# Moving 212 Strassen weight sums from GpSimd to VectorE, with a reordered opening and three re-placed pieces of vector work

## The chip, the cores and the metric

The program runs on one core of a Trainium2 chip. The metric is the device time of one execution in microseconds, the median of several runs. The engines are TensorE (PE, with its weight loads as PEld), VectorE (DVE), ScalarE (ACT) and GpSimd (POOL); SyncE (SP) only issues DMA. Each engine runs its own instructions in order and waits on semaphores of the others.

## The reference

One inference step of a one-layer encoder, float32, on 1,024 prompt tokens and 32 sample tokens (1,056 together, each 1,024 wide), and 256 memory tokens. Cut to its stages:

```python
def encoder_layer(h, ...):
    u = rms_norm(h, norm1)
    z = u @ w_in + b_in                       # q, k, v, gates of three branches
    o_h = hgrn2_recurrence(...)               # 4 heads, normed, gated
    h_m = mlstm_recurrence(q, k, v, i_pre, log_sigmoid(f), ...)   # 4 heads
    p = softmax(einsum(q_x, mem_k) * XA_DH ** -0.5)   # 4 heads, 256 memory tokens
    merged = sum of sigmoid(gate_b) * (branch_b @ w_branch[b])
    h = h + merged @ w_out
    up_g, up_v = split(rms_norm(h, norm2) @ w_up)     # 2 x 2,816
    conv = causal depthwise conv of width 3 over up_g
    h = h + (gelu(conv) * up_v) @ w_down
y = rms_norm(h, final_norm)
mem_k, mem_v = split(rms_norm(mem, mem_norm) @ w_mem_kv)
m_t = max over time of the mLSTM's running exponents  # the "rows" below
```

## The kernel before, in words

Activations lie transposed: channels on the 128 partitions, the 1,056 tokens as four column quarters of 264. Every product is three matmuls (`mm3`, L221 to L223): hi by hi, lo by hi and hi by lo, where `split` (L225) makes the hi part of an operand by an ACT cast (L226) and the lo part by a DVE subtraction (L227).

The large projections (`w_in` as `z_m1_m2`, `w_up` as `u0` to `u21`) use Strassen's scheme: seven products of 2x2 blocks in place of eight. For one pair of weight column blocks `operands` (L250) loads four weight quarters (L214, issued by SP into a ring of four buffers), forms four sums of them (`add`, L258) and splits the seven operands. 53 such sets give 212 sums. `seven` (L289) runs the products in the order 1, 2, 6, 5, 7, 3, 4 and adds them up from PSUM on ACT (L307, L309) and DVE (L311). The token side has the same seven operands (`put`, `put_sums`, L344 to L368), made once for `u1` (the normed input) and once for `n2` (the normed residual).

The stages in order of time: memory keys and values (`pm`, L527, eight weight blocks `wm0` to `wm7`) and, among them, the token norm with its transposes (`xp`, L469); the first z pairs (`z_35`, `z_33`) with cross-attention; HGRN2; the mLSTM's rows (`mlstm_rows`, L1043: 4x1056 scans over time on DVE) while gate projections run; the mLSTM heads; branch projections and gates; `wout_job` (L1294), which adds each block to the residual `acc` (L1317), squares it (L1322) and sums the squares (`sq`, L1323); `rstd_cols` (L317), whose matmuls `n21b` (L329) read `sq`; the up stage with a depthwise conv (L1371, L1374) and a gate product on POOL (`vt`, L1377, L1378), stored to DRAM as `h_d`; `down` (L1469), which loads `h_d` back (`hr`, L1462), splits it into `h` and multiplies by `w_down` (`pd`); the final norm.

The order of the work comes from `Flow` (L62): a clock kept by hand in which `fl.unit` adds the planned TensorE time of a piece, and generators (`x_norm`, `mlstm_rows`, the norms) are resumed when the clock has passed the wait that their `yield` names. `prep` and `ahead` (L195, L199) set how many weight operands are made ahead. The text is written in that order, and from it the instructions of each engine get a fixed order.

## Time and profile before

| what | value |
|---|---|
| median of 3 runs | 1861.42 us (1857.13 to 1862.22) |
| the profiled execution | 1859.81 us |
| its span | 1857.9 us |
| PE busy in the span | 1803.6 us (97%) |
| DVE, ACT, POOL busy | 1177.4, 842.6, 490.6 us |
| mean granted clock | 0.989 |

The span runs from the first to the last instruction of the profiled execution; 1.9 us of that execution's time lie around it. Busy time counts an engine's instructions; idle time of PE is put down to the instruction on another engine that released it last. The granted clock is a share of the full 2.4 GHz: 1.00 is that, 0.50 is 1.2 GHz, and a window between has some of both.

### The profile page before, as it was taken

Reading aid. Unit: us, or ns where it says so; the run is one execution under the profiler, and the core shown is the slowest. Engines: PE = TensorE matmul, PEld = TensorE weight load, DVE = VectorE, ACT = ScalarE, POOL = GpSimd, SP = SyncE. Lnnn points to the kernel's source line nnn. Section 1 sums busy time; section 2 is a strip of 40 time slices with the busy share of each in tenths; the row PEclk is TensorE's granted clock in tenths of the full one; section 3 lists DMA queues with packets and bytes.
Section 4 is the critical chain, followed back from the end, with each engine's and each line's share of the span. In section 5 each row is a group of like instructions: output and inputs, shape, how many; then the busy total and the mean of one; then the engine's idle time right before and its main releaser. Section 6 shows DMA issues by size and latency. Waiting matters only on the chain.

```text
span 1857.9 us, 35747 instructions
## 1 busy us (share of the span) xinstructions
PE 1803.6 (97%) x14249; PEld 1770.5 (95%) x14249; DVE 1177.4 (63%) x2265; ACT 842.6 (45%) x1779; POOL 490.6 (26%) x535
## 2 busy tenths in 40 slices
...
GB/s 299 43 53 64 87 57 64 62 55 55 81 86 111 57 67 66 62 79 206 320 384 248 119 106 67 98 70 87 72 84 70 87 78 127 287 146 144 133 97 127
DMA packets 99687, 213.95 MB, mean 115 GB/s; under 512 B 10788, under 2 KB 34724, under 8 KB 99520
## 3 DMA queue, kind: packets, MB, share of 16 engines
...
## 4 chain that ended last, share of the span: by engine, by line
PE 86%; DVE 7%; DMA 2%; ACT 2%; issue 1%; POOL 1%; SPq 0%; DVEq 0%; ACTq 0%; POOLq 0%
PE pd L221 4%; PE pd L222 4%; PE pd L223 4%; PE pb L222 2%; PE pb L223 2%; PE pb L221 2%; PE po L221 1%; PE po L222 1%; PE po L223 1%; DMA hr<-h_d 1%; DMA mems<-in_mem 1%; DMA wm<-in_w_mem 0%; PE fin L806 0%; PE z_55c0q L221 0%; PE z_2c0q L221 0%
## 5 line engine op out<-in xcount | busy, mean ns | idle before, releaser
L1377 POOL TENSOR_TENSOR vt<-cv,vt 128x1024 f32<-128x1024 f32 x22 | 53.4, 2425 | 107.3 <-ACT cv L1376 107.3
L1374 DVE SCALAR_TENSOR_TENSOR cv<-cb,par,cv 128x1058 f32<-128x1058 f32 x44 | 61.3, 1392 | 1.4
L1273 DVE TENSOR_TENSOR g<-pb,g 128x352 f32<-128x352 f32 x72 | 37.0, 521 | 23.8 <-PE pb L223 18.2
L527 PE MATMUL pm<-memg,wm 128*128 128x256 f32 x128 | 31.7, 398 | 9.4 <-DVE memg L427 7.9
L227 DVE TENSOR_TENSOR h<-hr,h 128x528 fp32r<-128x528 f32 x44 | 31.7, 746 | 13.0 <-ACT h L226 12.6
L527 PEld LDWEIGHTS pm<-memg,wm 128*128 128x128 f32 x128 | 24.5, 199 | 12.9 <-DVE memg L427 7.9
L325 POOL MEMSET fn11rs<- 128x3 f32 x1 | 0.1, 100 | 131.7 <-DVE fn00a L175 131.7
L226 ACT CAST h<-hr 128x528 fp32r<-128x528 f32 x44 | 26.5, 631 | 17.5 <-DMA hr<-h_d 15.2
L1448 POOL TENSOR_TENSOR y<-y,fn10b 128x264 f32<-128x264 f32 x4 | 3.8, 980 | 110.5 <-ACT fn10b L1442 110.5
L611 ACT ACTIVATE gt<-gt 128x1056 f32<-128x1056 f32 x24 | 26.0, 1088 | 10.8 <-DVE gt L311 10.8
L1275 DVE TENSOR_TENSOR old<-old,g 128x352 f32<-128x352 f32 x48 | 25.1, 523 | 6.0 <-DMA old<-part 5.1
L612 POOL DMA_DIRECT2D g_d<-gt x24 | 13.4, 557 | 50.3 <-ACT gt L611 47.7
L1322 ACT ACTIVATE sqt<-acc 128x264 f32<-128x264 f32 x28 | 11.8, 423 | 32.0 <-DVE acc L1317 29.5
L1376 ACT ACTIVATE cv<-cv 128x1058 f32<-128x1058 f32 x22 | 24.0, 1090 | 4.0 <-DVE cv L1374 2.0
L226 ACT CAST mgh<-old 128x264 fp32r<-128x264 f32 x32 | 12.4, 412 | 27.9 <-DVE old L1275 27.9
L1325 POOL DMA_DIRECT2D h_d<-acc x8 | 6.1, 759 | 71.9 <-DVE acc L1317 71.9
L1317 DVE TENSOR_TENSOR acc<-acc,po 128x264 f32<-128x264 f32 x32 | 13.6, 424 | 16.9 <-PE po L223 16.9
L1517 DVE TENSOR_TENSOR y<-y,pd 128x264 f32<-128x264 f32 x32 | 12.7, 426 | 10.1 <-PE pd L223 10.1
L1371 DVE TENSOR_SCALAR cv<-cb,par 128x1058 f32<-128x1058 f32 x22 | 18.5, 841 | 0.1
L1367 POOL COPY ffo<-cb 128x2 f32<-128x2 f32 x22 | 5.5, 252 | 45.7 <-DVE cb L311 45.7
L1323 DVE TENSOR_TENSOR sq<-sq,sqt 128x264 f32<-128x264 f32 x28 | 13.2, 473 | 6.3 <-ACT sqt L1322 6.3
L1531 ACT ACTIVATE fqt<-y 128x264 f32<-128x264 f32 x28 | 11.3, 419 | 12.9 <-DVE y L1517 12.9
...
## 6 DMA issues: line engine op xcount, KB each, us to landing
...
```

The lines of the kernel that those rows point to most:

```text
L221: PE.matmul(out, lh, rh, start=first and i == 0, stop=False, skip_group_check=part)
L222: PE.matmul(out, lh, rl, start=False, stop=False, skip_group_check=part)
L223: PE.matmul(out, ll, rh, start=False, stop=last and i == n - 1, skip_group_check=part)
L226: S.copy(hi, src)
L227: V.tensor_tensor(out=lo, in0=src, in1=hi.bitcast(F32), op=ALU.subtract)
L527: PE.matmul(ps[:, 0:NM], w[:, 4 * a + k], mg[a][:, k], start=a + k == 0, stop=a + k == 4)
L611: S.activation(t, t, AF.Sigmoid)
L1273: V.tensor_tensor(out=gt[:, c], in0=ps[:, 0:GW], in1=gt[:, c], op=ALU.mult)
L1275: V.tensor_tensor(out=old[:, c], in0=old[:, c], in1=gt[:, c], op=ALU.add)
L1374: V.scalar_tensor_tensor(out=cv, in0=cb[:, tap:tap + n], scalar=col(C_CW + tap * NF + i), in1=cv, op0=ALU.mult, op1=ALU.add)
L1376: S.activation(cv, cv, AF.Gelu_apprx_tanh)
L1377: G.tensor_tensor(out=vt[:, 0:TP], in0=cv[:, 0:TP], in1=vt[:, 0:TP], op=ALU.mult)
```

## The change

Five edits.

1. `add` issues its 212 additions on VectorE (`V`) where it used GpSimd (`G`).
2. The opening's loads on SP go in another order: first x0, the gain row and x1, then the halves of memT and wm0, then x2 to x4, wm1, x5 to x8, wm2, the two blocks of memory rows, wm3 and on. Squares, reciprocal roots and scaling of the token rows (`x_scale`) are written where the rows are loaded, not one chunk after another in `x_norm`.
3. `mlstm_rows` is cut by seven `yield`s, so that other work may stand between its steps, and begins later in the planned clock (9.0 in place of 3.0).
4. The operands of the first up block (`u0`, first half) are registered inside the loop over `wout_job`, at its sixth block of the second half, with homes of their own for both raw weights; its last two operands are registered behind the loop.
5. In `down` the `hr` loads of the next three steps are issued ahead of the weight loads, and the residual loads (`y`) come at step 4 and not at step 0.

The core of the diff:

```diff
         def add(n, a, b, out=None):
...
-            G.tensor_tensor(out=out, in0=a, in1=b, op=ALU.add)
+            V.tensor_tensor(out=out, in0=a, in1=b, op=ALU.add)
             return out
...
+                            if i in homes:
                                 if not kh:
-                                    t = other[0](f"{nm}r1").bitcast(F32)
+                                    t = homes[i](f"{nm}r{i}").bitcast(F32)
                                 raws[i, kh] = t[:, kh * HK:(kh + 1) * HK]
                                 nc.sync.dma_start(raws[i, kh], src)
...
             return go
-        first = [prep(1 if n >= len(other) else 0.25, make(p)) for n, p in enumerate(ORD)][0]
-        return first, ops
...
+        entries = []
+        def register(part):
+            entries.extend(prep(1 if n >= len(other) else 0.25, make(ORD[n])) for n in part)
+        register(range(7 if later is None else len(other)))
+        if later is not None:
+            later.append(lambda: register(range(len(other), 7)))
+        return entries, ops
...
+    LOADS = ((2, 3, 4), (5, 6, 7, 8), (9, 10)) + ((),) * 5
...
                 nc.sync.dma_start(t, I["w_mem"][i])
-                for j in ((), (2, 3, 4), (5, 6), (7, 8))[i] if i < 4 else ():
-                    x_load(j)
-                if i == 2:
-                    for j in range(2):
-                        nc.sync.dma_start(mem_s[j], I["mem"][j * P:(j + 1) * P])
+                for j in LOADS[i]:
+                    load_rows(j)
+                for j in LOADS[i]:
+                    if j < NC:
+                        x_scale(j)
...
             nc.scalar.dma_start(par, I["par"])
             x_load(0)
+            grow.append(slot("grow", F32)[:, 0:D])
+            nc.sync.dma_start(grow[0], I["g1"].broadcast_to([P, D]))
+            x_load(1)
             for a in range(2):
                 c = slice(a * HK, (a + 1) * HK)
                 nc.sync.dma_start(mem_f[a], I["memT"][a])
                 nc.sync.dma_start(t[:, c], I["w_mem"][0][:, c])
-            grow.append(slot("grow", F32)[:, 0:D])
-            nc.sync.dma_start(grow[0], I["g1"].broadcast_to([P, D]))
-            x_load(1)
+            for j in LOADS[0]:
+                load_rows(j)
+            for j in (0, 1, *LOADS[0]):
+                x_scale(j)
             fl.start(x_norm(), 0.0, key="u")
...
+    def x_scale(i):
+        n = CHUNKS[i][1]
+        if not xss:
+            xss.append(mp.tile([P, 16], F32, tag="ssn", name="xss", bufs=3))
+            G.memset(xss[0], 1.0)
+        ss, x = xss[0], x_t[i]
+        junk = mp.tile([P, D], mybir.dt.bfloat16, tag="pe", name=f"junk{i}", bufs=4)
+        S.activation(junk[:n], x[:n], AF.Square, accum_out=ss[:n, i:i + 1])
+        y = rsqrt(ss[:, i:i + 1], 1, f"x{i}", 1.0 / D)
+        V.scalar_tensor_tensor(out=x[:n], in0=x[:n], scalar=y[:n, 0:1], in1=grow[0][:n], op0=ALU.mult, op1=ALU.mult)
...
         for i, (t0, n) in enumerate(CHUNKS):
             x = x_t[i]
-            junk = mp.tile([P, D], mybir.dt.bfloat16, tag="pe", name=f"junk{i}", bufs=4)
-            S.activation(junk[:n], x[:n], AF.Square, accum_out=ss[:n, i:i + 1])
-            y = rsqrt(ss[:, i:i + 1], 1, f"x{i}", 1.0 / D)
-            V.scalar_tensor_tensor(out=x[:n], in0=x[:n], scalar=y[:n, 0:1], in1=grow[0][:n], op0=ALU.mult, op1=ALU.mult)
-            yield 0.0, 1.6, None
             for kh in range(2):
...
         S.activation(e, e, AF.Ln, bias=1.0)
+        yield 0.0, 6.5, None
         V.scalar_tensor_tensor(out=x, in0=x, scalar=0.0, in1=e, op0=ALU.min, op1=ALU.subtract)
...
         V.memset(e[:, TP:TP + 1], 0.0)
+        yield 0.0, 2.0, None
         b = rr
         V.tensor_tensor_scan(out=b, data0=e, data1=lf, initial=0.0, op0=ALU.mult, op1=ALU.add)
+        yield 0.0, 2.4, None
         V.tensor_tensor_scan(out=m[:, 0:TP], data0=lf[:, 0:TP], data1=i_[:, 0:TP], initial=0.0,
                              op0=ALU.add, op1=ALU.max)
+        yield 0.0, 3.3, None
         V.tensor_tensor_scan(out=m[:, TP:T], data0=lf[:, TP:T], data1=i_[:, TP:T],
                              initial=par[0:H, C_SM:C_SM + 1], op0=ALU.add, op1=ALU.max)
         V.tensor_copy(outm[:, 0:1], m[:, TP - 1:TP])
...
         V.tensor_tensor(out=rows[0:H], in0=i_, in1=b, op=ALU.subtract)
+        yield 0.0, 1.3, None
         V.tensor_tensor(out=rr, in0=b, in1=m, op=ALU.subtract)
         nc.gpsimd.dma_start(rd_d, rr)
+        yield 0.0, 1.3, None
         r3 = rr[:, 0:TP].rearrange("p (c t) -> p c t", t=P)
         m3 = m[:, 0:TP].rearrange("p (c t) -> p c t", t=P)
...
+        yield 0.0, 2.4, None
...
-            yield 0.0, 3.0, None
+            yield 0.0, 9.0, None
...
-    for cp in range(2):
-        for j in range(KD):
-            wout_job(cp, j)
...
+    def up_reg(i, cp, other=(), homes={}, later=None):
+        return operands(f"u{i}c{cp}", I["w_up"][i], I["w_up"][NF + i], up_tile, other, homes, later)
+    later = []
+    for cp in range(2):
+        for j in range(KD):
+            if (cp, j) == (1, 5):
+                reg0 = up_reg(0, 0, [slot] * 5, {0: slot, 1: slot}, later)
+            wout_job(cp, j)
+    later[0]()
...
-    up_job(0, (0,), up_reg(0, 0, [slot] * 5))
-    reg1 = up_reg(1, 0, [jrow] * 3)
+    up_job(0, (0,), reg0)
+    reg1 = up_reg(1, 0, [jrow] * 3, {1: jrow})
...
         for n, (cp, g, k, kk) in enumerate(seq):
             w = DG[cp][0][1]
             ms, qs = MG[cp][g]
+            for c, gr, kh, _ in seq[n:n + 3]:
+                if gr == 0 and (c, kh) not in hs:
+                    hload(c, kh)
             while at < min(len(seq), n + 3):
-                if seq[at][1] == 0 and (seq[at][0], seq[at][2]) not in hs:
-                    hload(seq[at][0], seq[at][2])
                 ws[seq[at]] = wload(*seq[at])
                 at += 1
             if k == 0:
                 if g == 0:
-                    ys = {}
-                    sq = [None, None]
-                    for m0 in range(0, KD, 2):
-                        t = jt(f"y{cp}{m0}", 4 * w).rearrange("p (m s t) -> p m s t", m=2, s=2)
-                        nc.sync.dma_start(t.rearrange("p m s t -> p m (s t)"),
-                                          h1_d[m0:m0 + 2, :, DG[cp][0][0]:DG[cp][0][0] + 2 * w].rearrange("m p t -> p m t"))
-                        ys[m0], ys[m0 + 1] = t[:, 0], t[:, 1]
+                    ys, sq = {}, [None, None]
                 pss = {(m, s): (gbank if s else bank)(f"pd{cp}{m}{s}") for m in ms for s in qs}
+            if (g, k) == (0, 4):
+                for m0 in range(0, KD, 2):
+                    t = jt(f"y{cp}{m0}", 4 * w).rearrange("p (m s t) -> p m s t", m=2, s=2)
+                    nc.sync.dma_start(t.rearrange("p m s t -> p m (s t)"),
+                                      h1_d[m0:m0 + 2, :, DG[cp][0][0]:DG[cp][0][0] + 2 * w].rearrange("m p t -> p m t"))
```

How the instructions stand now, at the three places that follow. TensorE at the end of the opening, before (`pm` are the memory products, `pmt` and `xp` transposes, `z_35c0q` the first product of the z pairs):

```order
L527 MATMUL pm_460<-memg_93,wm_289 128x256 x4
L494 MATMUL pmt_477<-ident,kvol 128x128 x2
L527 MATMUL pm_460<-memg_94,wm_289 128x256 x4
L469 MATMUL xp_487<-ident,x_180 128x128 x4
L469 MATMUL xp_493<-ident,x_180 128x128 x4
L527 MATMUL pm_506<-memg_93,wm_352 128x256 x4
L494 MATMUL pmt_523<-ident,kvol 128x128 x2
L527 MATMUL pm_506<-memg_94,wm_352 128x256 x4
L469 MATMUL xp_534<-ident,x_182 128x32 x4
L469 MATMUL xp_540<-ident,x_182 128x32 x4
L221 MATMUL z_35c0q_572<-u101h,z_35c0o_413 128x264
```

and after:

```order
L554 MATMUL pm_456<-memg_93,wm_327 128x256 x4
L554 MATMUL pm_456<-memg_94,wm_327 128x256 x4
L554 MATMUL pm_498<-memg_93,wm_364 128x256 x4
L521 MATMUL pmt_507<-ident,kvol 128x128 x2
L554 MATMUL pm_498<-memg_94,wm_364 128x256 x4
L554 MATMUL pm_524<-memg_93,wm_401 128x256 x4
L521 MATMUL pmt_529<-ident,kvol 128x128 x2
L554 MATMUL pm_524<-memg_94,wm_401 128x256 x4
L554 MATMUL pm_551<-memg_93,wm_454 128x256 x4
L521 MATMUL pmt_561<-ident,kvol 128x128 x2
L554 MATMUL pm_551<-memg_94,wm_454 128x256 x4
L221 MATMUL z_35c0q_594<-u101h,z_35c0o_495 128x264
```

The nine chunks' transposes (`xp`) stood between the memory products down to the last row ahead of `z_35`; now the last of them stands ahead of all these rows, which hold the last four of the eight blocks of `pm`.

VectorE at the mLSTM's rows, before (lines L1058 to L1075 are the recurrence, `gt` a gate tile that L311 brings out of PSUM, `z_43c0o` operands of the next gate block):

```order
L1058 SCALAR_TENSOR_TENSOR rr<-mt_6249,mt_6194 4x1056
L1059 SCALAR_TENSOR_TENSOR mr<-mt_6194,mif 4x1024
L1061 SCALAR_TENSOR_TENSOR mr<-mt_6194,par,mif 4x32
L1063 COPY outm<-mr 4x1
L1066 TENSOR_TENSOR rows<-mif,rr 4x1056
L1064 COPY outm<-mr 4x1
L311 TENSOR_TENSOR gt_6197<-gt_6197,z_41c0q_6201 128x264
L1067 TENSOR_TENSOR rr<-rr,mr 4x1056
L311 TENSOR_TENSOR gt_6197<-gt_6197,z_41c0q_6215 128x264
L1073 COPY mt_6249<-rr 4x128
L1074 TENSOR_TENSOR mt_6249<-rr,mr 4x896
```

and after (L318 is the former L311, L259 the sums, L1087 to L1107 the former L1058 to L1074):

```order
L318 TENSOR_TENSOR gt_6197<-gt_6197,z_41c0q_6215 128x264
L1080 SCALAR_TENSOR_TENSOR mt_6194<-mt_6194,mt_6310 4x1056
L227 TENSOR_TENSOR z_43c0o_6339<-z_43c0r_6331,z_43c0o_6339 128x512
L227 TENSOR_TENSOR z_43c0o_6368<-z_43c0r_6333,z_43c0o_6368 128x512
L318 TENSOR_TENSOR gt_6196<-gt_6196,z_41c0q_6295 128x264
L318 TENSOR_TENSOR gt_6196<-gt_6196,z_41c0q_6317 128x264
L1082 MEMSET mt_6310 4x1056
L227 TENSOR_TENSOR z_43c0o_6405<-z_43c0s_6403,z_43c0o_6405 128x512
L1083 MEMSET mt_6310 4x8
L1084 MEMSET mt_6310 4x1
L259 TENSOR_TENSOR z_43c0s_6403<-z_43c0s_6403,z_43c0r_6333 128x512
L1087 SCALAR_TENSOR_TENSOR rr<-mt_6310,mt_6194 4x1056
```

Three scans (L1058 to L1061) and a 4x1056 difference stood ahead of the evacuation of `gt_6197`; now `gt_6197` and `gt_6196` both come out ahead of the first scan (L1087), and splits and a sum stand between the steps.

VectorE at the end of the output projection, before (`sq` is the running sum of squares, `u0c0o` and `u1c0o` operands of the up stage):

```order
L1323 TENSOR_TENSOR sq<-sq,sqt_12695 128x264
L227 TENSOR_TENSOR u1c0o_12809<-u1c0r_12802,u1c0o_12809 128x512
L1317 TENSOR_TENSOR acc_12150<-acc_12150,po_12731 128x264
L227 TENSOR_TENSOR u1c0o_12812<-u1c0r_12804,u1c0o_12812 128x512
L227 TENSOR_TENSOR u0c0o_12720<-u0c0s_12718,u0c0o_12720 128x512
L227 TENSOR_TENSOR u0c0o_12723<-u0c0s_12716,u0c0o_12723 128x512
L227 TENSOR_TENSOR u0c0o_12728<-u0c0s_12726,u0c0o_12728 128x512
L1323 TENSOR_TENSOR sq<-sq,sqt_12757 128x264
L1317 TENSOR_TENSOR acc_12152<-acc_12152,po_12761 128x264
L227 TENSOR_TENSOR u0c0o_12796<-u0c0s_12718,u0c0o_12796 128x512
L227 TENSOR_TENSOR u0c0o_12799<-u0c0r_12707,u0c0o_12799 128x512
L1323 TENSOR_TENSOR sq<-sq,sqt_12787 128x264
```

and after (L1357 is the former L1323, L1351 the former L1317):

```order
L1357 TENSOR_TENSOR sq<-sq,sqt_12722 128x264
L259 TENSOR_TENSOR u0c0s_12494<-u0c0s_12494,u0c0r_12480 128x512
L1351 TENSOR_TENSOR acc_12150<-acc_12150,po_12737 128x264
L227 TENSOR_TENSOR n204l<-acc_11604,n204h 128x1056
L227 TENSOR_TENSOR u0c0o_12731<-u0c0s_12494,u0c0o_12731 128x512
L227 TENSOR_TENSOR u0c0o_12734<-u0c0r_12483,u0c0o_12734 128x512
L1357 TENSOR_TENSOR sq<-sq,sqt_12763 128x264
L1351 TENSOR_TENSOR acc_12152<-acc_12152,po_12767 128x264
L1357 TENSOR_TENSOR sq<-sq,sqt_12793 128x264
```

From the third last `sq` to the last there were nine rows besides the second last `sq`, seven of them splits of `u0` and `u1`; now there are six, two of them splits of `u0`, one a sum and one a split of the norm's operands (`n204l`), which stood earlier before.

## Rows read from the trace of the kernel before

**Rows 1.** The page: its first line and the busy time of each engine

```profile
span 1857.9 us, 35747 instructions
...
PE 1803.6 (97%) x14249; PEld 1770.5 (95%) x14249; DVE 1177.4 (63%) x2265; ACT 842.6 (45%) x1779; POOL 490.6 (26%) x535
```

**Rows 2.** The waits of PE: whom for, us in total, times, longest us

```profile
PE pm L527 <- DVE memg L427: 7.9, 1, 7.9
...
PE z_41c0q L221 <- DVE gt L311: 5.9, 1, 5.9
...
PE n21b L329 <- DVE sq L1323: 4.0, 2, 3.3
...
PE u0q L221 <- DVE vt L311: 2.8, 1, 2.8
...
PE pd L221 <- ACT h L226: 2.4, 1, 2.4
```

**Rows 3.** Windows of later stages, all engines (columns in the first line)

```profile
core 0: us, PE busy (x) PEld busy (x) DVE busy (x) ACT busy (x) POOL busy (x), PEclk, DMA share, GB/s
...
350.00:400.00 50.00, 49.25 (x390) 47.05 (x389) 44.51 (x106) 25.61 (x56) 16.88 (x15) 1.00 0.19 64
...
550.00:560.00 10.00, 4.07 (x23) 3.85 (x21) 10.00 (x12) 2.98 (x3) 6.39 (x5) 0.73 0.17 54
...
1120.00:1125.00 5.00, 5.00 (x26) 4.96 (x26) 4.30 (x10) 1.98 (x5) 3.39 (x4) 0.54 0.15 55
...
1165.00:1170.00 5.00, 4.79 (x26) 4.79 (x27) 4.96 (x7) 1.68 (x4) 5.00 (x4) 0.66 0.46 152
...
1200.00:1250.00 50.00, 50.00 (x415) 50.00 (x414) 31.78 (x44) 19.26 (x40) 23.33 (x28) 1.00 0.24 81
...
1590.00:1595.00 5.00, 3.55 (x18) 3.55 (x19) 3.54 (x6) 3.70 (x7) 0.00 (x0) 0.72 1.04 372
```

**Rows 4.** Windows, line L258 alone: POOL busy (count), clock, DMA share, GB/s

```profile
0.00:1858.00 1858.00, 293.76 (x212) 0.99 0.34 115
```

**Rows 5.** Groups by line and shape, DVE L227: busy us, mean ns, idle

```profile
L227 DVE TENSOR_TENSOR u10c0o<-u10c0s,u10c0o 128x512 fp32r<-128x512 f32 x4 | 3.8, 955 | 3.4 <-ACT u10c0o L226 3.4
...
L227 DVE TENSOR_TENSOR z_15c0o<-z_15c0s,z_15c0o 128x512 fp32r<-128x512 f32 x4 | 2.7, 679 | 0.0
```

**Rows 6.** Timeline of POOL, one set of the up stage: start, us, idle before

```profile
1300.79 1.35 POOL L258 TENSOR_TENSOR u9c0s<-u9c0r,u9c0r 128x512 f32<-128x512 f32 x1 [4.02 <-DMA u9c0r<-in_w_up]
```

**Rows 7.** Windows of the opening, columns as in rows 3

```profile
0.00:50.00 50.00, 36.45 (x191) 30.96 (x192) 29.61 (x87) 30.64 (x72) 8.42 (x22) 1.00 0.75 280
...
50.00:60.00 10.00, 8.22 (x61) 7.14 (x60) 10.00 (x13) 8.34 (x16) 3.33 (x3) 1.00 0.38 132
...
60.00:70.00 10.00, 6.11 (x41) 5.10 (x39) 10.00 (x12) 5.56 (x9) 0.00 (x0) 0.82 0.02 5
...
70.00:80.00 10.00, 8.32 (x52) 7.90 (x53) 9.59 (x10) 6.83 (x9) 3.90 (x2) 0.84 0.10 28
```

**Rows 8.** Timeline of PE, the first matmul of z_35

```profile
53.77 0.39 PE L221 MATMUL z_35c0q<-u101h,z_35c0o 128*128 128x264 f32 x1
```

**Rows 9.** The chain that ended last: start us, us, what

```profile
13.93 10.17 DMA mems<-in_mem
...
1583.50 7.24 DMA hr<-h_d
```

**Rows 10.** Timeline of DVE at three places: start us, us, instruction

```profile
549.83 3.29 DVE L1059 TENSOR_TENSOR_SCAN mr<-mt,mif 4x1024 f32<-4x1024 f32 x1
...
556.51 0.41 DVE L311 TENSOR_TENSOR gt<-gt,z_41c0q 128x264 f32<-128x264 f32 x1
...
1112.12 3.83 DVE L227 TENSOR_TENSOR u0c0o<-u0c0s,u0c0o 128x512 fp32r<-128x512 f32 x3
...
1117.76 1.66 DVE L1323 TENSOR_TENSOR sq<-sq,sqt 128x264 f32<-128x264 f32 x1
...
1294.45 2.21 DVE L227 TENSOR_TENSOR u8c0o<-u8c0r,u8c0o 128x512 fp32r<-128x512 f32 x1 [1.34 <-ACT u8c0o L226]
```

More of the change, by code (lines that the diff above doesn't have):

```diff
@@ L248, in stream_step, with operands @@
     ORD = (1, 2, 6, 5, 7, 3, 4)
-    def operands(nm, w1, w2, tiles=optile, other=()):
+    def operands(nm, w1, w2, tiles=optile, other=(), homes={}, later=None):
         raws, sums, ops = {}, {}, {}
@@ L266, in go @@
                             src = w[:, kh * HK:(kh + 1) * HK]
-                            if i and other:
+                            if i in homes:
                                 if not kh:
-                                    t = other[0](f"{nm}r1").bitcast(F32)
+                                    t = homes[i](f"{nm}r{i}").bitcast(F32)
                                 raws[i, kh] = t[:, kh * HK:(kh + 1) * HK]
@@ L285, in make, with seven @@
             return go
-        first = [prep(1 if n >= len(other) else 0.25, make(p)) for n, p in enumerate(ORD)][0]
-        return first, ops
-    def seven(nm, first, ops, ub, cps, dst, need, bias=(None, None), hook=None, keep=False):
+        entries = []
[5 more added lines that the diff above has]
+        return entries, ops
+    def seven(nm, entries, ops, ub, cps, dst, need, bias=(None, None), hook=None, keep=False):
         banks = {}
         for n, p in enumerate(ORD):
-            ahead(first + n, first if keep else None)
+            ahead(entries[n], entries[0] if keep else None)
             o = ops[p]
@@ L398, in stream_step, with load_rows @@
     bbm = mp.tile([P, NM], F32, tag="kc", name="bbm", bufs=1)
+    LOADS = ((2, 3, 4), (5, 6, 7, 8), (9, 10)) + ((),) * 5
+    NC = len(CHUNKS)
+    def load_rows(j):
+        if j < NC:
+            x_load(j)
+        else:
+            nc.sync.dma_start(mem_s[j - NC], I["mem"][(j - NC) * P:(j - NC + 1) * P])
     def mem_prep(i):
@@ L405, in go @@
                 nc.sync.dma_start(t, I["w_mem"][i])
-                for j in ((), (2, 3, 4), (5, 6), (7, 8))[i] if i < 4 else ():
-                    x_load(j)
-                if i == 2:
-                    for j in range(2):
-                        nc.sync.dma_start(mem_s[j], I["mem"][j * P:(j + 1) * P])
+                for j in LOADS[i]:
+                    load_rows(j)
+                for j in LOADS[i]:
+                    if j < NC:
+                        x_scale(j)
                 return
@@ L452, in x_load @@
         nc.sync.dma_start(x_t[i][:n], I["x"][i * P:i * P + n])
+    xss = []
+    def x_scale(i):
[8 more added lines that the diff above has]
+        V.scalar_tensor_tensor(out=x[:n], in0=x[:n], scalar=y[:n, 0:1], in1=grow[0][:n], op0=ALU.mult, op1=ALU.mult)
     def x_norm():
         b = {(q, kh): quads(slot(f"xb{q}{kh}", F32) if q % 2 else jt(f"xb{q}{kh}")) for kh in range(2) for q in range(4)}
-        ss = mp.tile([P, 16], F32, tag="ssn", name="xss", bufs=3)
-        G.memset(ss, 1.0)
         for i, (t0, n) in enumerate(CHUNKS):
             x = x_t[i]
-            junk = mp.tile([P, D], mybir.dt.bfloat16, tag="pe", name=f"junk{i}", bufs=4)
-            S.activation(junk[:n], x[:n], AF.Square, accum_out=ss[:n, i:i + 1])
-            y = rsqrt(ss[:, i:i + 1], 1, f"x{i}", 1.0 / D)
-            V.scalar_tensor_tensor(out=x[:n], in0=x[:n], scalar=y[:n, 0:1], in1=grow[0][:n], op0=ALU.mult, op1=ALU.mult)
-            yield 0.0, 1.6, None
             for kh in range(2):
@@ L559, in z_pair, with run @@
         for cps in part or ((0, 1),):
-            first, ops = operands(f"{nm}c{cps[0]}", I["w_in"][m1], I["w_in"][m2])
-            def run(cps=cps, first=first, ops=ops):
+            entries, ops = operands(f"{nm}c{cps[0]}", I["w_in"][m1], I["w_in"][m2])
+            def run(cps=cps, entries=entries, ops=ops):
                 if "t" not in at:
@@ L565, in run @@
                 t = at["t"]
-                seven(f"{nm}c{cps[0]}", first, ops, u1, cps, lambda m, q: [(slice(0, QW), t[m][:, qcols(q)])],
+                seven(f"{nm}c{cps[0]}", entries, ops, u1, cps, lambda m, q: [(slice(0, QW), t[m][:, qcols(q)])],
                       "u1", (col(C_BIN + m1), col(C_BIN + m2)), hook)
@@ L1346, in up_tile @@
         return mp.tile([P, T], F32R, tag="tot", name=name, bufs=2)
+    def up_reg(i, cp, other=(), homes={}, later=None):
[7 more added lines that the diff above has]
+    later[0]()
+    W_ = TP + 2
+    cbs, vts, hs = {}, {}, {}
     def up_begin(i):
```

14 lines of the change are left out of this document (1 added, 13 removed).

## The prediction

> **What bounds the kernel now.** I read the page first: TensorE is busy for 1803.6 of 1857.9 us [rows 1], so 54.3 us of idle time are all that a change to the other engines can return, apart from time that TensorE spends at its lower clock. In the list of TensorE's waits the reader is to see few, long ones: 7.9 us at the start, then 5.9, 4.0, 2.8 and 2.4 us, each at one place [rows 2]. The windows show what lies between these places: 50.00 of 50 us busy in the up stage and 49.25 in HGRN2 [rows 3]. There is nothing to gain in such a stretch, only something to lose. They also show that after a long wait TensorE's granted clock falls: 0.73, 0.54, 0.66 and 0.72 in windows behind the four waits [rows 3], where 0.50 is 1.2 GHz and 1.00 is 2.4. A wait that goes returns that as well. A fifth place is the opening: from 50 to 80 us TensorE is busy for 8.22, 6.11 and 8.32 of each 10 us, while VectorE shows 10.00, 10.00 and 9.59 [rows 7]. There VectorE is the bound. About 0.3% (5.6 us) is what a measurement of this kernel can tell from no change.
>
> **The sums (edit 1).** GpSimd spends 293.76 us on 212 of them, 1.39 us each [rows 4], and gets rid of it. VectorE does a 128x512 operation of two inputs in 0.68 us where GpSimd is quiet (a z set) and in 0.96 us where it is not (an up set) [rows 5]. So VectorE takes on 212 x 0.68 = 144 us. In return its own operations run undisturbed: 4 x 0.28 = 1.1 us for the sum operands of an up set, and more for single ones. Its busy share rises from 63% to some 66 to 70%. Two rows show how the disturbance works: a split that began at 1294.45 us took 2.21 us, a `sq` addition of 264 columns at 1117.76 us took 1.66 us [rows 10]. The Trainium skill says of this ("SBUF — State Buffer", section "Who interferes with whom") that a VectorE instruction with two SBUF inputs and a GpSimd one that reads SBUF exclude each other for a whole instruction. By that the added sums would meet GpSimd's remaining products (`vt`) as the splits did, which is a price in the up stage only.
>
> What does it cost on the path? In the up stage and in most z sets nothing: VectorE has 18 of 50 us free in the up stage, 5.5 of 50 in HGRN2 [rows 3]. But VectorE works in order, and the first sum waits for the last of four weight quarters: GpSimd waited 4.02 us for it in the set shown [rows 6], and the same wait now holds up what stands behind it on VectorE, evacuations among it. What of that reaches TensorE no row shows. The bounds are 0, as in the up stage, where the next evacuation is some us later, and 0.6 us a set, about one operation. I take 0.1 us for each of 30 z sets, near zero because 0.75 of 50 us is all that VectorE's nearly full stretch loses now [rows 3]: **+3 us**, with 0 and 18 as ends.
>
> **The opening (edit 2).** The first product of `z_35` begins at 53.77 us [rows 8]. Until then TensorE worked 36.45 us in the first 50 [rows 7] and, at 8.22 of 10, 3.1 us behind, 39.6 in all. From its first matmul at 7.9 us [rows 2] without a stop that is done at 47.5, so at most 6.3 us can go. The first matmul is now a transpose, which needs x0, the gain row and a square, a root and a scaling; the memory products come behind x1 and wait for 1 MB more. I put the start where it was. The memory rows, whose load ended at 13.93 + 10.17 = 24.1 us [rows 9], have two more x loads (0.6 MB) ahead; the window of the first 50 us moves 280 GB/s on average [rows 7], so that is 2 us, which other products cover. I take **-4 us**. Behind it lies the larger part: all transposes now stand ahead of the last four memory blocks, so the pieces on VectorE that make `u1`'s operands can begin some 10 us earlier: half of the memory products, which with the transposes fill the 39.6 us, now stand behind the last transpose (an estimate, 15 us at most), under matmuls that need little of VectorE. What they have to catch up with is, from 50 to 80 us, 30 - 22.65 = 7.35 us of idle time, and at 0.82 and 0.84 [rows 7] about 1.1 + 1.3 = 2.4 us of clock, 9.8 us. Against this stand eight sums of `z_35` and `z_33`, 8 x 0.68 = 5.4 us, on the engine that is the bound here. I take **-6 us**; the ends are -2 and -16 for both together.
>
> **The rows (edit 3).** TensorE waits 5.9 us for `gt` [rows 2], which left PSUM only at 556.51 us, behind three scans of up to 3.29 us [rows 10]. Now both tiles come out ahead of the first scan, and what can stand ahead of a later evacuation is one scan. The clock of 0.73 is 2.7 us in the window, part of it idle; 1.5 us is what working time lost. Of 7.4 us I take **-7**, with -3 as the end at which a single scan of 3.3 us still holds up one evacuation.
>
> **From output projection to up stage (edits 1 and 4).** Two waits for `sq`, 4.0 us [rows 2], and a clock of 0.54, 5 x 0.46 = 2.3 us [rows 3]. From 1112.12 us three splits of `u0` took 3.83 us where 3 x 0.68 = 2.0 is undisturbed, and the last `sq` took 1.66 us [rows 10] against the 0.41 us of an addition as wide in the same rows. This alone is 3 us; five of nine rows between the last sums of squares leave as well. I count 6.3 us as gone. The 2.8 us for `vt` and 5 x 0.34 = 1.7 of clock behind it [rows 2, 3] are not moved by the order, only by the absence of disturbance: I count half, 2.2 us. Moved forward, the splits and sums of `u0` stand between those of `wo15` and `wo16`, and the second half of `wo15` now comes behind two splits and a sum: 0.7 us lost. Sum: **-7.8 us**, with -3 and -11 as ends.
>
> **Down (edit 5).** TensorE waits 2.4 us for `h`, whose load took 7.24 us from 1583.50 [rows 2, 9], and loses 1.4 us at 0.72 [rows 3]. The load stood on SP behind the store of the last `vt` and four `y` loads. Now three such loads go ahead of that store, and the one behind it belongs to a step three pairs later. The `y` loads are needed only at the end of the pass. I take **-3.5 us**, with 0 as the end if the ring of buffers holds the loads back.
>
> **Sum.** -4 - 6 - 7 - 7.8 - 3.5 + 3 = -25.3 us. 1859.81 - 25.3 = 1834.5; the median stands 1.6 us above the profiled execution, so **1836 us**.
>
> **The rivals.** (a) *The next wait takes the place.* Behind each wait stands an in-order VectorE with another late row: a scan, `vt`, a split of `wo15`. Then half of the 28.3 us goes: 1861.4 - 14 + 3 = 1850 us. For it: the four places have different releasers [rows 2]. Against it: at three of them the rows that were late have left.
>
> (b) *The opening gives nothing back.* VectorE has 10.00 of 10 us there [rows 7], and the sums make it 5.4 us longer, so the 6 us of the second part fall to about 0 and the start gains 2: 1836 + 8 = 1844 us. The Trainium skill ("Perfetto Trace Analysis", section "Optimizing Scalar/DVE Operations") has a rule that speaks for it: where VectorE is saturated, work may well go to GpSimd, the reverse of edit 1. The rows agree that VectorE is saturated in this stretch, though not in the span as a whole (63%).
>
> (c) *Slower.* The wait for the fourth weight quarter, on VectorE in order, holds up evacuations in z sets, where VectorE is at 44.51 of 50 us [rows 3]. The place is HGRN2 and attention, 30 sets. At 0.94 us a set it eats the 28.3 us; at 1.2 us, a third of GpSimd's wait of 4.02 us, the time is 1861.4 - 28.3 + 36 = 1869 us.
>
> (d) *Nothing that can be measured.* The edits only shift which row is late, and the clock falls elsewhere: 1858 to 1864 us.
>
> **Chances.** Forecast 0.56, (a) 0.17, (b) 0.12, (d) 0.08, (c) 0.07. Of (a) some lies within 0.3%, so faster is 0.83, the same 0.10, slower 0.07. The range takes in (a) and (b) and the ends of the terms: with 16, 7.4, 10.8 and 3.8 us gone and no price for the sums the time is 1823, with all small ends but 3 us for the sums 1861.4 - 2 - 3 - 3 + 3 = 1856. I give 1824 to 1856.
>
> **What would show it.** In the profile after, GpSimd is near 200 us and VectorE near 1230 to 1320. The list of TensorE's waits no longer has `gt` at 5.9, `sq` at 4.0 or `h` at 2.4 us, and the clock is 1.00 in windows there. `z_35` begins near 50 us, and TensorE is busy for over 9 of 10 us from 50 to 80. The up stage stays at 50 of 50. The prediction is wrong if windows in HGRN2 fall below 48 of 50, or if waits for VectorE of over 2 us stand at the old places under another name.

## The result, and the profile after

The changed kernel takes 1833.05 us (median of 4 runs, 1831.32 to 1834.02), the kernel before beside it 1861.12 us: a ratio of 0.985, 95% interval 0.9834 to 0.9866, 28.1 us less. Forecast were 1836 us and a range of 1824 to 1856. The profiled execution took 1831.32 us. The page, first line and busy times, after [rows 1]:

```profile
span 1829.5 us, 35711 instructions
...
PE 1794.2 (98%) x14249; PEld 1763.2 (96%) x14249; DVE 1232.2 (67%) x2477; ACT 842.4 (46%) x1780; POOL 190.2 (10%) x323
```

The span is 28.4 us shorter: TensorE's idle time fell from 54.3 to 35.3 us (19.0 us), and its busy time from 1803.6 to 1794.2 us (9.4 us), with as many matmuls: fewer of them ran at 1.2 GHz, as the mean granted clock shows, 0.997 against 0.989. GpSimd has 300 us less, VectorE 55 us more. The list of TensorE's waits, against [rows 2] (whom for, us in total, times, longest):

```profile
PE xp L496 <- DVE x L486: 11.0, 2, 8.7
PE pm L554 <- DVE kvoh L533: 2.3, 1, 2.3
PE u2q L221 <- DVE vt L318: 1.8, 1, 1.8
...
PE u1q L221 <- DVE cb L318: 1.4, 1, 1.4
...
PE z_43c0q L221 <- DVE gt L318: 0.7, 1, 0.7
PE m0pi L1237 <- DVE m0nt L1244: 0.6, 1, 0.6
...
PE m1pi L1237 <- DVE m1nt L1244: 0.5, 1, 0.5
```

`gt`, `sq` and `h` are gone from the head of the list. In their place stand a wait for the first token rows, a longer one for `kvoh` (1.3 us before), waits of 1.4 to 1.8 us early in the up stage, and four of 0.3 to 0.6 us in the mLSTM heads (`m*pi`, two of them shown), which the kernel before did not have. The windows of the opening, against [rows 7], then two of HGRN2 and the up stage, against [rows 3]:

```profile
0.00:50.00 50.00, 35.71 (x185) 30.36 (x186) 34.52 (x91) 34.10 (x76) 4.35 (x19) 1.00 0.74 267
50.00:60.00 10.00, 10.00 (x67) 9.33 (x66) 9.93 (x16) 4.80 (x10) 1.07 (x2) 1.00 0.28 87
60.00:70.00 10.00, 8.89 (x66) 8.06 (x65) 8.69 (x12) 8.09 (x15) 0.00 (x0) 1.00 0.33 111
70.00:80.00 10.00, 9.96 (x80) 9.61 (x79) 9.95 (x15) 6.46 (x12) 0.00 (x0) 1.00 0.09 28
350.00:400.00 50.00, 50.00 (x414) 48.70 (x413) 44.61 (x107) 23.54 (x42) 5.36 (x5) 1.00 0.19 65
1200.00:1250.00 50.00, 50.00 (x414) 50.00 (x414) 36.02 (x55) 19.56 (x41) 7.34 (x14) 1.00 0.24 80
```

TensorE works for 28.85 of 30 us from 50 to 80, where it had 22.65, and at full clock. In HGRN2 it has 50.00 of 50 in place of 49.25. But it did less in the first 50 us, and `z_35` began later than before, not sooner [rows 8]:

```profile
55.08 0.47 PE L221 MATMUL z_35c0q<-u101h,z_35c0o 128*128 128x264 f32 x1
```

To see where time was won, the table takes the start of the same first matmul in each trace, and gives how much earlier it is than before (before at 130.47, 533.42, 583.33, 1014.77, 1331.13 and 1710.25 us; the last column is the span). A step between two columns is what that stage gained. Two traces of the same kernel (the first two rows) differ by up to 1.6 us in a step, so one step of one trace is no surer than that. The kernels below the second row are those of the experiments.

| kernel | z_0 | z_41 | z_16 | output proj. | u10 | first final norm | end |
|---|---|---|---|---|---|---|---|
| changed | 7.9 | 13.5 | 20.6 | 18.9 | 22.5 | 26.5 | 28.4 |
| after_again (the same) | 6.7 | 12.2 | 19.3 | 18.6 | 23.8 | 26.7 | 28.0 |
| e1_sums_pool | 3.8 | 2.5 | 9.0 | 8.7 | 5.7 | 9.3 | 10.7 |
| e2_open_old | 5.0 | 10.2 | 17.2 | 15.6 | 19.6 | 23.7 | 24.4 |
| e3_rows_old | 6.2 | 11.8 | 15.2 | 14.6 | 20.0 | 24.1 | 24.0 |
| e4_up_old | 5.5 | 11.1 | 18.2 | 17.3 | 23.1 | 27.1 | 30.1 |
| e5_down_old | 6.7 | 12.3 | 19.4 | 18.7 | 22.7 | 23.8 | 24.1 |
| e6_sums_only | 3.9 | 9.0 | 12.5 | 10.7 | 18.0 | 18.9 | 18.8 |

In the changed kernel the opening gave 7.9 us, attention and HGRN2 (z_0 to z_41) 5.6, the rows 7.1, the mLSTM heads lost 1.7, the way from output projection to up stage gave 3.6, down 4.0 and the end 1.9.

### The profile page after: what moved, and what is told of

Read it like the earlier page. It is cut to its first block, busy times and chain, and to the rows that moved or that the text cites. A ratio compares the mean times of both kernels' runs of the same rounds, so it can differ in the third digit from the quotient of the medians.

```text
span 1829.5 us, 35711 instructions
## 1 busy us (share of the span) xinstructions
PE 1794.2 (98%) x14249; PEld 1763.2 (96%) x14249; DVE 1232.2 (67%) x2477; ACT 842.4 (46%) x1780; POOL 190.2 (10%) x323
## 4 chain that ended last, share of the span: by engine, by line
PE 65%; DVE 2%; DMA 1%; issue 1%; ACT 0%; POOL 0%; DVEq 0%; SPq 0%; ACTq 0%
PE pd L221 5%; PE pd L223 5%; PE pd L222 5%; PE pb L221 3%; PE pb L223 3%; PE pb L222 3%; PE po L221 2%; PE po L223 2%; PE po L222 2%; PE z_45c0q L221 0%; PE z_30c0q L221 0%; PE z_29c0q L221 0%; PE z_31c0q L221 0%; PE z_47c0q L221 0%; PE u10q L222 0%
## 5 line engine op out<-in xcount | busy, mean ns | idle before, releaser
L227 DVE TENSOR_TENSOR h<-hr,h 128x528 fp32r<-128x528 f32 x44 | 31.8, 749 | 13.7 <-ACT h L226 13.3
L226 ACT CAST h<-hr 128x528 fp32r<-128x528 f32 x44 | 26.5, 633 | 16.5 <-DMA hr<-h_d 14.2
L638 ACT ACTIVATE gt<-gt 128x1056 f32<-128x1056 f32 x24 | 26.2, 1090 | 12.0 <-DVE gt L318 11.8
L554 PEld LDWEIGHTS pm<-memg,wm 128*128 128x128 f32 x128 | 24.4, 200 | 6.5 <-DVE kvoh L533 2.5
L1351 DVE TENSOR_TENSOR acc<-acc,po 128x264 f32<-128x264 f32 x32 | 13.5, 426 | 18.3 <-PE po L223 18.3
L226 ACT CAST mgh<-old 128x264 fp32r<-128x264 f32 x32 | 12.5, 413 | 27.8 <-DVE old L1309 27.8
L496 PE MATMUL xp<-ident,x 128*128 128x128 f32 (+1 forms) x72 | 11.2, 302 | 11.8 <-DVE x L486 11.0
L496 PEld LDWEIGHTS xp<-ident,x 128*128 128x128 f32 (+1 forms) x72 | 9.4, 159 | 13.4 <-issue 8.6
L1548 DVE TENSOR_TENSOR y<-y,pd 128x264 f32<-128x264 f32 x32 | 12.7, 427 | 10.2 <-PE pd L223 10.2
L1414 DVE TENSOR_SCALAR cv<-cb,par 128x1058 f32<-128x1058 f32 x22 | 18.2, 827 | 0.1
L1357 DVE TENSOR_TENSOR sq<-sq,sqt 128x264 f32<-128x264 f32 x28 | 12.0, 430 | 6.5 <-ACT sqt L1356 6.5
L227 DVE TENSOR_TENSOR mgl<-old,mgh 128x264 fp32r<-128x264 f32 x32 | 13.2, 428 | 4.4 <-ACT mgh L226 4.3
```

The lines of the kernel that those rows point to most:

```text
L226: S.copy(hi, src)
L227: V.tensor_tensor(out=lo, in0=src, in1=hi.bitcast(F32), op=ALU.subtract)
L554: PE.matmul(ps[:, 0:NM], w[:, 4 * a + k], mg[a][:, k], start=a + k == 0, stop=a + k == 4)
L638: S.activation(t, t, AF.Sigmoid)
```

## The experiments

There are twelve runs on three chips; each time stands beside runs of the kernel before on the same chip, and ratios are to those. The same kernel's ratio moved from 0.985 to 0.9826 between two chips, some 4 us, so differences below that are read from the table of marks or from runs on one chip.

**The sums back on GpSimd.** Edit: `V.tensor_tensor` in `add` is `G.tensor_tensor` again, all else as changed.

> The changed kernel with its 212 sums back on GpSimd, all else as changed. Theory (VectorE's own operations are what gains, as they run undisturbed): 5 to 9 us slower than the changed kernel's 1833, so 1838 to 1842; 128x512 splits near 0.96 us in the up stage again, a little idle time of TensorE in HGRN2 (49.2 of 50 us from 350 to 400), and a wait for sq or vt of 1 us or more behind the output projection. Rival (the sums' place is indifferent, the placements do it all): 1831 to 1835. Second rival (the sums hold VectorE up): 2 us or more faster than 1833, with the waits of 0.3 to 0.6 us for m*nt in the mLSTM gone.

Measured: 1846.27 us, ratio 0.9921 (0.9908 to 0.9933): 13 us slower than the changed kernel by the ratios. More than expected, and the rivals are out. The marks put the loss in the opening (4 us), in attention and HGRN2 (7 us) and on the way to the up stage (7 us). All `L227` operations together, and one set of the up stage, first in e1, then in the changed kernel, as [rows 5] has it before (columns of the first line of each: busy us, count, clock, DMA share, GB/s):

```profile
0.00:1900.00 1900.00, 535.46 (x694) 0.99 0.33 113
```
```profile
L227 DVE TENSOR_TENSOR u10c0o<-u10c0s,u10c0o 128x512 fp32r<-128x512 f32 x4 | 3.8, 952 | 3.4 <-ACT u10c0o L226 3.4
```
```profile
0.00:1900.00 1900.00, 493.83 (x694) 1.00 0.33 113
```
```profile
L227 DVE TENSOR_TENSOR u10c0o<-u10c0s,u10c0o 128x512 fp32r<-128x512 f32 x4 | 2.8, 689 | 0.5 <-ACT u10c0o L226 0.5
```

The 694 low parts cost 41.6 us more while GpSimd makes the sums; in this set a split takes 0.95 us against 0.69. VectorE as a whole is busy for 1172.1 us in e1 and 1232.2 in the changed kernel, of which the sums are 145.2: its other work is 85 us shorter. That the two engines exclude each other can be read from pairs of rows. Here a split of e1 begins 0.12 us behind a sum on GpSimd and ends 0.55 us behind its end:

```profile
1146.30 1.29 POOL L259 TENSOR_TENSOR u0c1s<-u0c1s,u0c1r 128x512 f32<-128x512 f32 x1 [12.54 <-issue]
```
```profile
1146.42 1.72 DVE L227 TENSOR_TENSOR u0c1o<-u0c1s,u0c1o 128x512 fp32r<-128x512 f32 x1
```

Of e1's 478 splits of 128x512, the 95 that overlap a sum on GpSimd take 1.07 us on average. The 360 that overlap no two-input operation of GpSimd take 0.69, as the 455 such splits of the changed kernel do.

**The sums alone.** Edit: that one line, in the kernel before.

> The kernel before with edit 1 alone: the 212 sums on VectorE, every other edit left out. Theory (the sums are the larger part, as putting them back cost the changed kernel 13 us): 11 to 15 us faster than the kernel before, 1846 to 1850; the wait for sq under 1 us, that for gt about 3 us, that for h still 2.4. Rival (the parts only work together): less than 8 us faster, 1853 or more.

Measured: 1840.47 us, ratio 0.9883 (0.9867 to 0.9899), 21.7 us less: more than the theory's 11 to 15, and the rival is out. This line by itself gives what would be three quarters of the change. But edits 2 to 5 without it (e1) give 14.2 us, and the two together 28.1, not 35.9: in part they remove the same waits. The waits of e6:

```profile
PE pd L221 <- ACT h L226: 2.9, 1, 2.9
PE z_41c0q L221 <- DVE gt L311: 2.9, 1, 2.9
PE u2q L221 <- DVE vt L311: 2.2, 1, 2.2
```

The wait for `sq` is gone without edit 4, and that for `gt` has fallen from 5.9 to 2.9 us without edit 3; `h` is still there (2.9 us, 2.4 before). From z_41 to z_16 it gains 3.5 us, half of what the changed kernel gains there.

**The opening in the old order.** Edit: `mem_prep`, `x_load` and `x_norm` as before.

> The changed kernel with the opening's loads and token scaling in the old order. Theory (VectorE is late for u1's operands because the last transposes stand behind all memory products): 6 to 9 us slower than 1833, so 1839 to 1842, first z_35 matmul near 53.8 us, and 5 to 8 us of idle time from 54 to 90 us. Rival (the sums on VectorE, undisturbed, gave that back, the order does nothing): 1831 to 1835, TensorE busy for over 9 of 10 us from 50 to 80 us in the old order too.

Measured: 1835.23 us, ratio 0.9864 (0.9851 to 0.9877). Neither side holds as a whole: the time is 2.2 us longer, within what two chips differ by, but the old stall is still there:

```profile
51.47 0.39 PE L221 MATMUL z_35c0q<-u101h,z_35c0o 128*128 128x264 f32 x1
```
```profile
50.00:60.00 10.00, 9.20 (x70) 8.16 (x69) 10.00 (x16) 7.28 (x14) 1.07 (x2) 1.00 0.36 118
60.00:70.00 10.00, 6.29 (x34) 5.37 (x33) 10.00 (x11) 4.95 (x7) 0.00 (x0) 0.83 0.01 4
70.00:80.00 10.00, 8.71 (x69) 8.51 (x70) 9.96 (x13) 7.14 (x12) 0.00 (x0) 1.00 0.07 24
```

The old order starts `z_35` 3.6 us sooner than the changed kernel and then waits for VectorE, full for 30 us. At z_0 the two kernels with the old order (e2, e6) have gained 4.5 us on average; six traces with the new one and quiet sums have 5.5 to 7.9, 6.6 on average. Some 2 us is what edit 2 gives beside edit 1, where I had 10; with the sums on GpSimd (e1) it gives 3.8.

**The rows in one piece.** Edit: the seven `yield`s out, 3.0 in place of 9.0.

> The changed kernel with the mLSTM's rows in one piece again. Theory: the wait for gt of 5 to 6 us returns near 540 us, with half clock behind it: 7 us slower than 1833, near 1840. Rival (the old wait was long because GpSimd disturbed the scans): a wait of 2 to 3 us and 1835 to 1837.

Measured: 1834.38 us, ratio 0.9856 (0.9842 to 0.9869). The wait is there, at the rival's size:

```profile
PE z_41c0q L221 <- DVE gt L318: 2.9, 1, 2.9
```

Between z_41 and z_16 it gains 3.5 us; every kernel with edit 3 and quiet sums gains 7.1. This does not make the two worth half each. In e1, where the rows are cut and GpSimd makes the sums, the stage gains 6.5 us, and all that is left of the wait for `gt` on VectorE, 5.9 us before, is this:

```profile
PE z_43c0q L221 <- DVE gt L318: 1.1, 1, 1.1
```

The cut alone takes nearly all of the wait away, the quiet GpSimd alone half of it, and together they gain hardly more than the cut. In the whole time 1.3 us are left, less than two chips differ by; the marks behind it (down to u10) give some back.

**u0 registered behind the output projection.** Edit:

```diff
-            if (cp, j) == (1, 5):
-                reg0 = up_reg(0, 0, [slot] * 5, {0: slot, 1: slot}, later)
             wout_job(cp, j)
-    later[0]()
+    reg0 = up_reg(0, 0, [slot] * 5, {1: slot})
```

> The changed kernel with u0's operands registered behind the output projection again. Theory (the order of the splits and the last sq is what took the wait away): a wait for sq of 2 us or more near 1090 us and 1836 to 1838. Rival (the quiet GpSimd alone did it, since the splits take 0.68 us each): no wait over 1 us there, 1831 to 1834.

Measured: 1829.4 us, ratio 0.9829 (0.9815 to 0.9842). It is faster than the changed kernel, which neither side had. To settle it both ran on one chip:

> e4_up_old once more beside the changed kernel on one chip. Theory (registering u0 inside the output projection costs, since its splits and sums stand between those of the last output weights): 2 to 4 us faster than the changed kernel. Rival (the first measurement was the scatter between chips): within 1 us.

> The changed kernel once more, beside the next one on the same chip: 1831 to 1835. It is the yardstick for e4_up_old, e10 and e11, which differ by a few us.

Measured: 1828.47 us (1827.38 to 1829.83) against 1830.54 us (1828.26 to 1832.36). The ratios, 0.9819 (0.9805 to 0.9832) and 0.9826 (0.9812 to 0.984), overlap: 2.1 us by medians, not settled by time. The marks say the same in five kernels with edit 4 and quiet sums and three without: from output projection to u10 the first gain 3.6, 4.0, 5.5, 4.0 and 5.2 us, the others 5.9, 6.1 and 7.2. The clearest step is from the output projection to the first matmul of `u2` (at 1162.00 us before): the five gain 3.3 to 3.5 us there, the three 5.3 each. What scatters lies behind it: from `u2` to u10 the traces with a stretch of half clock near 1162 us gain 0.3 to 0.8 us, those without it (after_again, e3, e6) 1.9 to 2.0. Edit 4 takes back about 2 us. VectorE in e4_up_old, before `u2`'s wait of 2.2 us for `vt`, and GpSimd beside it:

```profile
1156.43 0.69 DVE L259 TENSOR_TENSOR u3c0s<-u3c0r,u3c0r 128x512 f32<-128x512 f32 x1 [0.52 <-DMA u3c0r<-in_w_up]
1157.16 2.75 DVE L259 TENSOR_TENSOR u3c0s<-u3c0s,u3c0r 128x512 f32<-128x512 f32 x1
...
1160.48 0.41 DVE L318 TENSOR_TENSOR vt<-vt,u2q 128x264 f32<-128x264 f32 x1
```
```profile
1156.54 2.83 POOL L1418 TENSOR_TENSOR vt<-cv,vt 128x1024 f32<-128x1024 f32 x1 [5.75 <-ACT cv L1417]
```

The sums of `u3` stand ahead of the evacuation of `vt`. The first waits for its weight quarter, the second meets GpSimd's product, takes 2.75 us and ends 0.54 us after the product does, the third follows, and only then comes `vt`.

**Down in the old order.** Edit: the loop of `down` as before.

> The changed kernel with the loads of the down stage in the old order. Theory: the wait for h near 1566 us returns (2 to 2.5 us) with 1 to 1.7 us of half clock behind it: 1836 to 1837 against the changed kernel's 1833. Rival (the store of the last vt now comes sooner, so its queue is no longer late): no wait, 1832 to 1834.

Measured: 1834.56 us, ratio 0.985 (0.9836 to 0.9865), which is the changed kernel's ratio.

```profile
PE pd L221 <- ACT h L226: 2.7, 1, 2.7
```

The wait returns, as the theory had it, and between u10 and the final norm it gains 1.1 us where kernels with edit 5 gain 2.8 to 4.1. The time itself does not show these 2.7 us.

**GpSimd busy, but not with the sums.** Edit: behind each sum on VectorE

```diff
+            junk = mp.tile([P, NM * 2], mybir.dt.bfloat16, tag="pjunk", ..., bufs=1)
+            G.tensor_tensor(out=junk, in0=out, in1=out, op=ALU.add)
```

> The changed kernel with one added GpSimd operation behind each of the 212 sums: it adds the sum to itself into a tile that nobody reads. VectorE still makes the sums; GpSimd reads as much of the memory as it did before. Theory (what the sums on GpSimd cost was that they held up VectorE's two-input operations): most of the 13 us come back, 1841 to 1847, with 128x512 splits above 0.85 us in the up stage. Rival (the cost was that a sum takes 1.39 us on GpSimd against 0.68, so operands were late): 1832 to 1836.

**Sums twice as long, GpSimd quiet.** Edit: ahead of each sum

```diff
+            V.tensor_tensor(out=out, in0=a, in1=a, op=ALU.max)
```

> The changed kernel with an added 128x512 operation of VectorE in front of each sum, whose output the sum overwrites, so that a sum takes 1.3 us on VectorE, as it took 1.39 on GpSimd, and GpSimd stays quiet. Theory (GpSimd's disturbance was the cost of the old sums, not that they came late): 1833 to 1838, though VectorE is busy for 130 us more. Rival (late operands were the cost): 1842 or more.

Measured: 1884.49 us, ratio 1.0122 (1.0106 to 1.0137), and 1880.07 us, ratio 1.0096 (1.0082 to 1.0109). Both are some 50 us slower than the changed kernel, so by their totals they tell nothing apart, and both expectations are missed. By stages they do. Attention and the larger part of HGRN2 in four kernels (e1, then e8, e11 and changed):

```profile
100.00:200.00 100.00, 95.37 (x759) 90.49 (x757) 74.08 (x167) 65.49 (x169) 29.26 (x27) 1.00 0.19 67
200.00:500.00 300.00, 297.63 (x2429) 287.00 (x2429) 221.59 (x504) 139.62 (x294) 82.95 (x73) 1.00 0.18 64
```
```profile
100.00:200.00 100.00, 94.36 (x739) 89.48 (x738) 81.02 (x177) 63.93 (x166) 25.05 (x27) 0.98 0.18 62
200.00:500.00 300.00, 293.65 (x2388) 285.13 (x2387) 242.87 (x542) 137.91 (x291) 79.81 (x72) 0.99 0.18 64
```
```profile
100.00:200.00 100.00, 98.30 (x781) 93.55 (x779) 82.88 (x196) 65.92 (x171) 10.79 (x14) 1.00 0.21 77
200.00:500.00 300.00, 299.14 (x2463) 290.34 (x2463) 257.62 (x597) 143.94 (x302) 22.64 (x29) 1.00 0.18 64
```
```profile
100.00:200.00 100.00, 98.03 (x781) 93.71 (x780) 77.69 (x193) 64.91 (x169) 10.71 (x14) 1.00 0.21 76
200.00:500.00 300.00, 299.89 (x2471) 291.35 (x2470) 229.58 (x543) 143.27 (x302) 22.46 (x29) 1.00 0.19 63
```

Where GpSimd is busy TensorE loses 7 us (e1) or 12 (e8) of these 400; where the sums are longer and GpSimd quiet it loses 2.6, and the changed kernel 2.1, though VectorE is then fullest of all (340 us in e11). And in e11 the sums come later still: the last sum of a z set ends 1.8 us behind the set's first matmul (the median of 14 sets), in e1 0.1 us behind. So ahead of the up stage the disturbance was the cost, not the sums' lateness. (In e8 the added operations follow VectorE's sums directly and so meet the next rows more often than the old sums did, 127 of 478 splits against 95; its 12 us are no measure of the old cost.)

In the up stage both lose 1 to 2 us a set, for another reason. In e11 the added operation needs one weight quarter alone, and stands ahead of an evacuation that TensorE waits for; 18 up blocks wait 1.2 to 2.0 us each for `cb` (start, us, idle before):

```profile
1401.84 0.69 DVE L259 TENSOR_TENSOR u14c0s<-u14c0r 128x512 f32<-128x512 f32 x1 [1.58 <-DMA u14c0r<-in_w_up]
1402.45 0.48 DVE L319 TENSOR_TENSOR cb<-cb,u12q 128x232 f32<-128x232 f32 x2
```

In e8 VectorE waits for the last quarter, and then the sums and splits take 1.5 us each beside GpSimd's added operations, with `vt`'s evacuation behind them:

```profile
1207.17 0.69 DVE L259 TENSOR_TENSOR u4c0s<-u4c0r,u4c0r 128x512 f32<-128x512 f32 x1 [4.53 <-DMA u4c0r<-in_w_up]
...
1208.51 1.53 DVE L259 TENSOR_TENSOR u4c0s<-u4c0r,u4c0r 128x512 f32<-128x512 f32 x1
1209.96 1.52 DVE L227 TENSOR_TENSOR u4c0o<-u4c0r,u4c0o 128x512 fp32r<-128x512 f32 x1
...
1212.85 0.42 DVE L320 TENSOR_TENSOR vt<-vt,u3q 128x264 f32<-128x264 f32 x1
```

In the changed kernel the same row of `vt` follows 3.1 us behind the first sum (1298.62 and 1301.76 us in its own trace), here 5.7 (another block). So the in-order wait that rival (c) named is real, and the up stage has less than about 2.6 us a set to spare for it; what it would do with lateness alone these runs don't tell.

**Five sets on GpSimd.** Edit, on e4_up_old: `G` for the sums of `u3`, z_29, z_30, z_31 and z_47, `V` for the other 48 sets.

> The kernel with u0 registered late (e4_up_old, 1829.4) with the sums of five of the 53 sets on GpSimd: u3, and the four sets whose first sum stands in front of the mLSTM's m*nt (z_29, z_30, z_31, z_47). Theory (a sum on VectorE that waits for its weight quarter, or for GpSimd's product, holds the evacuation behind it): the waits for vt at u2 (2.2 us, with 1.7 of clock) and for m*nt (0.2 to 0.3 us each) go, 1825 to 1827. Rival (GpSimd's sums slow VectorE as much as they free it): 1829 to 1832, a wait of over 1.5 us at u2 or u3.

Measured: 1827.34 us, ratio 0.9811 (0.9796 to 0.9825). Half of the theory holds: the waits of the mLSTM heads go (its marks from z_16 to the output projection gain 0.4 us where e4_up_old loses 0.9). `u2`'s wait stays, at 2.7 us:

```profile
1157.28 1.09 DVE L227 TENSOR_TENSOR u3c0o<-u3c0s,u3c0o 128x512 fp32r<-128x512 f32 x1 [4.07 <-ACT u3c0o L226]
1158.29 0.76 DVE L319 TENSOR_TENSOR vt<-vt,u2q 128x264 f32<-128x264 f32 x2
```

A split of `u3` still stands ahead of `vt`, and now waits 4.07 us for ScalarE's cast of a sum that GpSimd makes. That the order would have to change, and not the engine, is my reading; no run tries it.

**Memory rows loaded sooner.** Edit, on e9_five_sets_pool: `LOADS = ((2, 3, 4), (9, 10, 5, 6), (7, 8))` and `mem_rstd` begun at block 2. The wait that it is after, in the changed kernel: two `u1` sums stand in front of `kvoh`, whose evacuation frees the bank that `pm` waits for.

```profile
37.88 2.42 DVE L364 TENSOR_TENSOR xb<-xb,xb 128x1056 f32<-128x1056 f32 x2
40.21 1.08 DVE L533 TENSOR_TENSOR kvoh<-pm,bbm 128x256 f32<-128x256 f32 x3
```

> e9_five_sets_pool (1827.3) with the two memory-row loads ahead of x5 to x8 and their square roots begun one block sooner. Theory (the wait of 2.3 us for kvoh near 38 us, and the half clock of 3.4 to 6.8 us behind it, come from the memory rows' root and from sums that stand in front of kvoh): the wait goes, the clock stays 1.00 there, 1823 to 1826. Rival (the opening is bound by VectorE's total up to z_33, so a wait that goes comes back at 60 to 75 us): 1826 to 1829, with z_33 beginning no earlier than 89 us.

Measured: 1827.45 us, ratio 0.9813 (0.98 to 0.9827). The rival holds to the letter: `kvoh` leaves the list, `z_35` begins at 51.46 us, and

```profile
PE z_35c0q L221 <- DVE x2q L319: 2.9, 1, 2.9
```
```profile
60.00:70.00 10.00, 6.97 (x45) 6.56 (x44) 9.58 (x12) 7.16 (x13) 0.00 (x0) 0.83 0.34 118
```

the 2.9 us come back in front of VectorE; z_33 begins at 89.41 us. e9 and e10 are the fastest of the twelve; e10 is 3.1 us below the changed kernel on the same chip (1827.45 against 1830.54, where one of the latter's five runs lies within the range of the former).

## Why the prediction was right

The time lies 3 us below the forecast, the sign and the size were right, and no rival came as a whole; of (a) there is a part, the waits of 1.4 to 1.8 us early in the up stage. Of the signs that I named two failed: `z_35` did not begin near 50 us, and from 60 to 70 us TensorE is busy for 8.89 us, not over 9. The parts were less right than the sum.

- **The bound.** Right: what was won is idle time at a few places and the clock behind it, 19.0 and 9.4 us, and the up stage stayed at 50.00 of 50.
- **The sums, +3 us.** Wrong in sign. I read 0.75 us of idle time in 50 in HGRN2 as slack that VectorE's new work could only eat; it was itself the work of GpSimd's disturbance (e1, with the sums back on GpSimd, has 49.23 of 50 there, the changed kernel 50.00), and z_0 to z_41 gained 5.6 us. The in-order wait showed only in the mLSTM heads (1.7 us here, 0.7 in the repeat) and at `u2`. The step that failed is the bound from below: "0, as in the up stage" left out a gain, though the 0.28 us a split stood in [rows 5].
- **The opening, -10 us.** It gained 7.9, but some 4.5 of that would come without edit 2. The first part (-4, `z_35` near 50 us) failed: I put the start "where it was". The first matmul did come at 8.66 us, but `x0`'s and `x1`'s scaling and then `memg` follow each other on VectorE, so the first memory product came at 14.71 us, not 7.89. The second part came out at 6.2 us of idle time and 2.4 of clock against 6 forecast. Rival (b), that the sums eat the gain on a full VectorE, fails on e1: with the sums on GpSimd the opening gains 4 us less. The rule that I cited for it is half of what that section of the Trainium skill ("Perfetto Trace Analysis", "Optimizing Scalar/DVE Operations") says: it goes on that moving work between these two engines might not help, since they share a read port. e1's 4 us agree with that half.
- **The rows, -7 us.** 7.1 measured, and by the mechanism that I named: e1 gains 6.5 by the order alone. What I left out is that the quiet GpSimd by itself shortens the old wait to 2.9 us (e3 and e6 gain 3.5 each), so the two terms do not add up.
- **Output projection to up stage, -7.8 us.** 3.6 measured. The waits for `sq` went as forecast, but edit 1 alone is enough for that (e6 gains 7.2 there). In e1, with edit 4 and the sums on GpSimd, they are gone too, but TensorE waits 2.8 us for `wo15` and 3.8 for `vt` instead. The loss of 0.7 us that I put on the moved splits of `u0` was mis-sized: edit 4 costs about 2 us (3.4 against 5.3 at `u2`), and it was not needed. And `vt` was half kept, as forecast, by another cause: a sum that meets GpSimd's product. The Trainium skill ("SBUF — State Buffer", section "Who interferes with whom") has the two excluding each other; the 2.75 us sum, which begins 0.62 us behind the product and ends 0.54 us behind its end, agrees.
- **Down, -3.5 us.** 4.0 by the marks, of which edit 5 is some 2.7. 1.9 us more came at the end, where a stretch of half clock is missing; after_again, e4 and e9 lack it too, e2, e3 and e5 don't. No edit accounts for that (e2 and e3 have edit 5 as e4 and e9 do); the cause stays open, and I count it as luck.

So the total was right in part by luck, because errors met: 6.3 us too much for the opening and the way to the up stage, against 7 us by which the sums' term missed (+3 forecast; 5.6 gained and 1.7 lost) and the 1.9 us at the end.
